# Latent attention: q up-projection in six full column tiles, rope on whole tiles, rope rows moved through memory

## Chip, cores, metric

The kernel runs on one core of a Trainium2 chip. The metric is the device time of one execution in microseconds (us). Three timed runs of the kernel before gave 1356.15, 1357.79 and 1358.18 us (median 1357.79). Engines: PE (TensorE) multiplies matrices into PSUM; DVE (VectorE), ACT (ScalarE) and POOL (GpSimd) work on elements; SP only issues DMAs here.

## The reference

One decoder block on x (1024 x 1024, float32): RMSNorm, one input projection, sliding-window attention A, latent attention B, gates and output projections, a residual, and a SwiGLU feed-forward. The change touches only B:

```python
cq = rmsnorm(q_lat, q_norm_g[l])                              # (S, 384)
qb = (cq @ w_uq[l]).reshape(B, S, MLA_HEADS, MLA_QK_DIM)      # 8 heads x 96
q_nope, q_rope = jnp.split(qb, [MLA_NOPE_DIM], axis=-1)       # 64 + 32
q_rope = apply_rope(q_rope, cos_b, sin_b)
ckv = rmsnorm(kv_lat, kv_norm_g[l])
kvb = (ckv @ w_ukv[l]).reshape(B, S, MLA_HEADS, MLA_NOPE_DIM + MLA_V_DIM)
k_nope, vb = jnp.split(kvb, [MLA_NOPE_DIM], axis=-1)
k_rope = apply_rope(k_r[:, :, None, :], cos_b, sin_b)[:, :, 0, :]   # one for all heads
o_b = mla_attention(q_nope, q_rope, k_nope, k_rope, vb)       # causal, scale 96 ** -0.5

def apply_rope(x, cos, sin):
    x1, x2 = jnp.split(x, 2, axis=-1)
    return jnp.concatenate([x1 * cos - x2 * sin, x2 * cos + x1 * sin], axis=-1)
```

## The kernel before, in words

**Arithmetic.** Every float32 operand of a matmul is kept as two parts, hi (rounded by ACT, L163) and lo = value - hi (DVE or POOL, L166), and a product is three matmuls (`mm3`, L172 to L174): hi by hi, hi by lo, lo by hi. One matmul has 128 x 128 weights and up to 512 moving columns.

**Stages.** Input projections; sixteen steps of sliding-window attention with the gate projection beside them; the latent attention; output projections with gates; `w_out`; the feed-forward. The change lies in the latent attention, from the last gate steps (L1049 on) to the last latent head.

**Latent attention before.** The normalised latents `lat` are transposed into `cq` (three tiles of 128 latent columns) and `ckv` (two). The rotated key part `krT` is copied into rows 64 to 127 of the three rotating key tiles `kT`; it stands there twice, in rows 64 to 95 and again in rows 96 to 127 (L692 to L695 write it twice). A head's 96 query columns are widened on the host to 128: 64 plain ones, the 32 rope ones, and the 32 rope ones with their halves swapped (`_layouts`, L1714). `prod_q(h, s)` (L1090) makes q of one head and one half s of the sequence: nine matmuls, one DVE multiplication by the table `rope_t` (1 in the plain rows, cos in rows 64 to 95, -sin and +sin in rows 96 to 127, all times the scale), then hi on ACT and lo on POOL. The score matmul over 128 rows adds the cos and the sin products, since the key stands twice. `prod_k(j, s)` (L1100) makes the plain key of two heads, `prod_v(b)` (L1111) v of all heads for one block.

**Order.** Before the loop: `prod_q(0, 0)`, `prod_q(0, 1)`, `prod_k(0, 0)`, `prod_k(0, 1)`, `scores(0)`, and eight `prod_v` with `scores(1)` after the fourth. The loop runs over 64 tiles t (8 heads x 8 query blocks, the blocks of a head in the order 2, 3, 6, 7, 0, 1, 4, 5; n = t mod 8 is the place in that order): `scores(t + 2)`, then `pv` of a pair that is due, then at n = 2 and 4 the two halves of `prod_q(h + 1)`, at n = 3 and 5 of odd heads the two halves of `prod_k((h + 1) // 2)`, then `transposes(t)`. `scores` (L1132) writes a PSUM tile of two banks (`scb`, two of them), DVE takes the row bound, ACT the exponential p, POOL the reciprocal and the scaling of p; `transposes` (L1159) turns p on PE into `pTb`, and ACT and DVE split it to `pth` and `ptl`; `pv` (L1174) multiplies with v. So q and k of later heads are PE work between the softmax steps of the current one. Late in the loop (t from 30 on) parts of the next stage are mixed in: `load_oa`, `split_oa`, `split_ob`, weights, and in the last head `mix_a`.

**Who decides the order.** Up to L1036 PE and SP follow the program as written. From there to the middle of the `w_out` stage a planner sets the order of each engine's instructions at compile time, by program order and by which operands and buffers it expects to be ready. At run time each engine and each DMA queue goes strictly in that order.

**Buffers.** `U` is a pool of 21 slots of 4 KB per partition (weights' raw and split tiles, p, pth, ptl, tables), `V` one of 17 slots of 8 KB (`cq`, `ckv`, `kT`, `vM`, `qT`, later `oaT`), `P1` four PSUM banks (q, k, v, pTb, ob, oA), `PX` the other four (gate sums, then the two score tiles). A new tile waits until the last reader of the slot's former tile is done. Weights come through a `Stream`: `load_to` issues the DMA, `conv_to` splits, `get` takes the tiles.

Of the kernel before, what the change touches and what calls it, by code (L numbers as in the profile page):

```python
# [8 lines left out]
F32 = mybir.dt.float32  # L9
# [8 lines left out]
P = 128  # L18
# [24 lines left out]
C_RT = QL  # L43
C_CKV = QL + 2 * ROPE_B
LAT = C_CKV + KVL
# [44 lines left out]
def hybrid_block_kernel(  # L90
# [94 lines left out]
    def half(s):  # L185
        return slice(512 * s, 512 * s + 512)
# [18 lines left out]
    h_d = dram.tile([NB, P, 2, 4, P], F32, name="h_d")  # L205
    q_d = dram.tile([2 * NB, P, 256], F32, name="q_d")
    lat_d = dram.tile([NB, P, LAT], F32, name="lat_d")
    gate_d = dram.tile([16, P, S], F32, name="gate_d")
# [47 lines left out]
    def uq_unit(j):  # L256
        def load():
            raw = U("wr", F32, (P, 2, 3, P))
            nc.sync.dma_start(raw, w_uq[j])
            return raw  # L260

        def conv(raw):
            ws = []
            for u in range(2):
                w = U("wuq", F32R, (P, 2, 3, P))
                split(w[:, 0], w[:, 1], raw[:, u])
                ws.append(w)
            return ws

        st.add(("uq", j), load, conv)  # L270

    uq_unit(0)
    wkv2 = []

# [16 lines left out]
    for k in range(2):  # L291
        ukv_unit(k)
    for j in range(1, 4):
        uq_unit(j)
    for nm, dp in (("oa", 0), ("oa", 1), ("oa", 2), ("ob", 0), ("ob", 1), ("oa", 3), ("ob", 2), ("ob", 3)):
# [97 lines left out]
    def halves(ap, hw):  # L393
        return ap.rearrange("p (h t d) -> p h t d", t=2, d=hw)
# [670 lines left out]
    gate_step()  # L1065
    rope_t = U("rope_t")
    nc.sync.dma_start(rope_t, c_rope_t)
    st.conv_to(st.index[("ukv", 1)])
    gate_step()
    kT = [hi_lo("kT") for _ in range(3)]  # L1070
    for s in range(2):
        pr = P1("krT", (HD, 4, P))
        for j in range(4):
            nc.tensor.transpose(pr[:, j], lat[4 * s + j][:, C_RT:C_CKV], ident)
        for hi, lo in kT:
            split(hi[64:128, half(s)], lo[64:128, half(s)], pr.rearrange("p b c -> p (b c)"))
    gate_step()
# [3 lines left out]
    wk, wv = wkv2  # L1081
    wuq = {0: st.get(("uq", 0))}

# [5 lines left out]

    def prod_q(h, s):  # L1090
        if s == 0:
            qT[h] = hi_lo("qT")
        w = wuq[h // 2][h % 2]
        ps = P1("q")
        mm3(ps, [((w[:, 0, k], w[:, 1, k]), (cq[k][0][:, half(s)], cq[k][1][:, half(s)])) for k in range(3)])
        qf = U("qf")
        nc.vector.tensor_tensor(qf[:, 0:512], ps, rope_t[:, half(s)], op=ALU.mult)
        split(qT[h][0][:, half(s)], qT[h][1][:, half(s)], qf[:, 0:512], nc.gpsimd)

    def prod_k(j, s):  # L1100
# [3 lines left out]
        for u in range(2):  # L1104
            hi, lo = kT[(2 * j + u) % 3]
            split(hi[0:64, half(s)], lo[0:64, half(s)], ps[64 * u:64 * u + 64])

    prod_q(0, 0)
    prod_q(0, 1)

    def prod_v(b):  # L1111
# [5 lines left out]
        split(vM[b][:, :, 0:HD], vM[b][:, :, HD:P], ps.rearrange("p (h d) -> p h d", d=HD))  # L1117

    prod_k(0, 0)
    prod_k(0, 1)  # L1120

# [149 lines left out]
    for t in range(NT):  # L1271
# [429 lines left out]
def _layouts(a):  # L1701
# [6 lines left out]
    def pairs(m):  # L1708
# [4 lines left out]
    uq = a["w_uq"].reshape(3, P, NH, QK)  # L1713
    uq = np.concatenate([uq, uq[..., 80:96], uq[..., 64:80]], axis=-1)  # L1714
    out = [("x", a["x"]), ("x_t", a["x"].reshape(NB, P, NK, P).transpose(0, 3, 2, 1)),
# [3 lines left out]
           ("w_kl", tiles(w[:, C_KVL:C_KR])), ("w_gt", pairs(w[:, C_GATE:])), ("sinks", a["swa_sinks"]),  # L1719
           ("q_g", a["q_norm_g"]), ("w_uq", uq.reshape(3, P, 4, 2, P).transpose(2, 1, 3, 0, 4)),  # L1720
           ("kv_g", a["kv_norm_g"]), ("w_ukv", a["w_ukv"])]
# [8 lines left out]
def _constants():  # L1730
# [13 lines left out]

    rt = np.concatenate([np.ones((64, S), np.float32), c.T, c.T, -s.T, s.T]).astype(np.float32) * np.float32(-SC_B)
    q = np.arange(P)[:, None]
# [35 lines left out]
```

## Time and profile before

| | before |
|---|---|
| median of three timed runs | 1357.79 us |
| profiled execution, first to last instruction | 1357.9 us |
| mean granted PE clock | 0.999 |
| instructions | 18990, of them 6600 matmuls |
| latent attention, first q matmul to last score matmul | 350.9 to 543.7 us |
| bytes moved by DMA | 202.25 MB |

In the lists of instructions each row has the start in us, the duration in us, engine, line, operation, output<-input, shapes, and in brackets the idle time of the engine just before it and what ended that. A matmul of 512 columns is listed with some 390 ns, but the next one starts about 226 ns later: it is the distance of starts that counts for PE. In the table by stretches, each engine's busy time is followed by the number of its instructions. Rows of a tile give minimum, median and maximum duration in ns.

### The profile page before, as it was taken

What the parts mean: (1) busy time and instruction counts of PE and PEld (TensorE: products, weight loads), DVE (VectorE), ACT (ScalarE), POOL (GpSimd) and SP (SyncE); (2) the same over time, 40 slices, a digit from 0 to 9 for tenths busy, and PEclk for the clock granted to TensorE, in tenths of its full rate; (3) what the DMA queues carried; (4) which work ended last, traced back from release to release, by engine and by line L of the source; (5) the groups of instructions that cost most, each with busy time, mean ns of one, the idle gap of its engine ahead of it and who ended that gap; (6) DMA issues with size and microseconds to landing.
All of it is one profiled execution on the core that took longest, in us unless ns stands there. A gap on an engine that the chain in (4) does not pass through costs nothing.

```text
span 1357.9 us, 18990 instructions
## 1 busy us (share of the span) xinstructions
PE 1338.8 (99%) x6600; PEld 1122.6 (83%) x6600; DVE 914.3 (67%) x1495; ACT 641.1 (47%) x1299; POOL 557.1 (41%) x610
## 2 busy tenths in 40 slices
PE   9999999999999999999999999999999999999997
PEld 6899878878888888888887888888888888888886
DVE  6868767776777787585448866666656654664862
ACT  7433767665567777651336232322332332644443
POOL 1115545553166554200031465766665551022521
PEclk9999999999999999999999999999999999999999
DMA  9454322335100110671243353644434425996504
GB/s 359 162 182 157 115 102 83 101 129 179 54 1 13 44 47 17 250 239 55 112 167 134 127 175 143 228 178 178 151 137 178 164 85 180 380 380 245 171 11 145
DMA packets 78239, 202.25 MB, mean 149 GB/s; under 512 B 8768, under 2 KB 15424, under 8 KB 78144
## 3 DMA queue, kind: packets, MB, share of 16 engines
q1 hardware_dynamic: 76704, 198.68, 41.2%
q10 hardware_dynamic: 1440, 2.36, 0.5%
q8 instruction: 52, 0.85, 0.2%
q14 instruction: 43, 0.35, 0.1%
HBM read 141.24 MB, written 59.77 MB: 148 GB/s over the span
## 4 chain that ended last, share of the span: by engine, by line
PE 79%; DVE 8%; ACT 4%; issue 3%; POOL 3%; DMA 2%; SPq 0%; POOLq 0%; ACTq 0%; DVEq 0%
PE fa L174 7%; PE fa L172 7%; PE fa L173 7%; PE fb L174 6%; PE fb L173 6%; PE fb L172 6%; PE fd L172 5%; PE fd L174 5%; PE fd L173 5%; PE xo L172 2%; PE xo L174 2%; PE xo L173 2%; PE pTb L1170 1%; PE oA L172 1%; PE oA L174 1%
## 5 line engine op out<-in xcount | busy, mean ns | idle before, releaser
L166 DVE TENSOR_TENSOR wl<-wr,wl 128x512 fp32r<-128x512 f32 x150 | 153.6, 1048 | 72.3 <-ACT wl L163 71.9
L166 DVE TENSOR_TENSOR lrv<-lr,lrv 128x1024 fp32r<-128x1024 f32 x77 | 104.9, 1396 | 48.6 <-ACT lrv L163 44.5
L163 ACT CAST lrv<-lr 128x1024 fp32r<-128x1024 f32 x77 | 80.1, 1052 | 94.1 <-PE fd L174 55.6
L172 PE MATMUL fd<-lrv 128*128 128x512 f32 x308 | 119.8, 389 | 0.0
L173 PE MATMUL fd<-lrv 128*128 128x512 f32 x308 | 119.8, 389 | 0.0
L174 PE MATMUL fd<-lrv 128*128 128x512 f32 x308 | 119.8, 389 | 0.0
L177 POOL TENSOR_TENSOR wr<-wr,sm 128x512 f32<-128x512 f32 (+1 forms) x38 | 46.4, 1229 | 150.8 <-DVE wl L166 117.2
L163 ACT CAST wl<-wr 128x512 fp32r<-128x512 f32 x150 | 86.9, 623 | 2.1 <-DVE wr L828 1.9
L304 POOL TENSOR_SCALAR ms<-ss 128x1 f32<-128x1 f32 x32 | 8.7, 271 | 189.8 <-ACT xn L1546 111.5
L166 DVE TENSOR_TENSOR wl<-sm,wl 128x512 fp32r<-128x512 f32 x60 | 47.2, 812 | 46.0 <-ACT wl L163 45.9
L174 PEld LDWEIGHTS fd<-lrv 128*128 128x128 f32 x308 | 57.8, 188 | 12.1
L173 PEld LDWEIGHTS fd<-lrv 128*128 128x128 f32 x308 | 57.8, 188 | 12.1
L172 PEld LDWEIGHTS fd<-lrv 128*128 128x128 f32 x308 | 57.8, 188 | 11.8
L1155 POOL TENSOR_TENSOR denb<-denb,neg_one 128x1 f32<-128x1 f32 x64 | 38.0, 594 | 69.2 <-ACT p L1154 56.8
L1154 ACT ACTIVATE p<-scb,nmb 128x384 f32<-128x384 f32 (+3 forms) x64 | 47.6, 744 | 38.4 <-DVE nmb L1153 36.5
L166 DVE TENSOR_TENSOR ptl<-pTb,pth 128x512 fp32r<-128x512 f32 (+2 forms) x96 | 50.5, 550 | 14.0 <-ACT pth L163 13.4
L1153 DVE CUSTOM_DVE_ANT_0 scb<-scb,mask 128x384 f32<-128x384 f32 (+3 forms) x64 | 48.5, 758 | 13.1 <-PE scb L1145 12.5
L1438 ACT ACTIVATE act<-sm 128x512 f32<-128x512 f32 x11 | 7.0, 633 | 104.9 <-DVE sm L180 104.9
L1156 POOL TENSOR_SCALAR p<-p,denb 128x384 f32<-128x384 f32 (+3 forms) x64 | 49.4, 773 | 6.3
L163 ACT CAST pth<-pTb 128x512 fp32r<-128x512 f32 (+2 forms) x96 | 43.3, 482 | 12.2 <-PE pTb L1170 11.6
L172 PE MATMUL fb<-t2h,wl 128*128 128x512 f32 x120 | 47.4, 395 | 0.0
L172 PE MATMUL fb<-t3h,wl 128*128 128x512 f32 x120 | 47.3, 394 | 0.0
(348 smaller groups left out, 4310.2 us busy)
## 6 DMA issues: line engine op xcount, KB each, us to landing
lr<-la_d SPq DMA_DIRECT2D x77, 256.0 KB, 5.4
wr<-in_w_gate_dram SPq DMA_DIRECT2D x22, 512.0 KB, 3.9
wr<-in_w_up_dram SPq DMA_DIRECT2D x22, 512.0 KB, 5.1
wd<-in_w_down_dram SPq DMA_DIRECT2D x22, 512.0 KB, 6.6
rb_d<-wd SPq DMA_DIRECT2D x22, 512.0 KB, 2.6
la_d<-sd SPq DMA_DIRECT2D x22, 512.0 KB, 5.3
lr<-rb_d SPq DMA_DIRECT2D x44, 256.0 KB, 5.4
lr<-in_w_down_dram SPq DMA_DIRECT2D x33, 256.0 KB, 5.8
```

Of the source, the lines that this page charges most:

```text
L163: i = nc.scalar.copy(hi, src)
L166: (eng or nc.vector).tensor_tensor(lo, src, hi.bitcast(F32), op=ALU.subtract)
L172: nc.tensor.matmul(ps, ah, bh, start=first and i == 0, stop=False, skip_group_check=go_on)
L173: nc.tensor.matmul(ps, ah, bl, start=False, stop=False, skip_group_check=go_on)
L174: nc.tensor.matmul(ps, al, bh, start=False, stop=last and i == n - 1, skip_group_check=go_on)
L177: eng.tensor_tensor(out, a, b, op=ALU.subtract)
L304: nc.gpsimd.tensor_scalar(ms, ss, 1.0 / width, EPS, op0=ALU.mult, op1=ALU.add)
L1153: nc.vector.tensor_tensor_reduce(s_, s_, m_, 1.0, -NEG, op0=ALU.add, op1=ALU.min, accum_out=nm)
L1154: nc.scalar.activation(p_, s_, AF.Exp, scale=-1.0, bias=nm, accum_out=den)
L1155: nc.gpsimd.tensor_tensor(den, den, neg_one[:, 0:1], op=ALU.pow)
L1156: nc.gpsimd.tensor_scalar(p[:, 0:w], p[:, 0:w], den, 0.0, op0=ALU.mult, op1=ALU.add)
L1170: nc.tensor.transpose(pp[:, i], p[:, blk(k0 + i)], ident)
```

## The change

The eight widened column tiles of the q up-projection become six full ones: two tiles (`w_rope`) hold the first and the second rope half of all eight heads (8 x 16 columns each), four hold the plain 64 columns of two heads each. Four `uq` units of weights become three; two of them are taken before the loop.

A new function `prod_rope(s)` computes the two rope tiles for a half of the sequence (two times nine matmuls), multiplies each on DVE by a cos and a sin table (two table tiles instead of one), subtracts and adds on POOL, splits into hi and lo (ACT, DVE), and stores them to a new buffer `qr_d` in device memory. `prod_q(j, s)` now makes the plain part of two heads: nine matmuls, hi with the scale on ACT, lo on DVE, 64 rows each. At s = 0 it also issues four DMAs, two for each head, that fetch the head's 2 x 16 rope rows from `qr_d` into rows 64 to 95 of its `qT`. Scores use 96 rows instead of 128; the key's rope part stands once.

The order before the loop becomes: `prod_rope(0)`, `prod_rope(1)`, `prod_k(0, 0)`, `prod_k(0, 1)`, `prod_q(0, 0)`, `prod_q(0, 1)`, five `prod_v`, `scores(0)`, three `prod_v`, `scores(1)`. In the loop `prod_q` runs at n = 2 and 4 of heads 0, 2 and 4 only.

```diff
-C_CKV = QL + 2 * ROPE_B
+C_CKV = QL + ROPE_B
...
+    qr_d = dram.tile([2, P, 2, S], F32, name="qr_d")
...
     uq_unit(0)
+    uq_unit(1)
...
     for k in range(2):
         ukv_unit(k)
-    for j in range(1, 4):
-        uq_unit(j)
+    uq_unit(2)
...
-        kr = t[:, C_RT:C_CKV].rearrange("p (u d) -> p u d", u=2)
-        rope_nat(halves(ps[:, QL:416], 16), 1, 16, rope_b[:, 0, b], rope_b[:, 1, b],
-                 [kr[:, 0:1].rearrange("p h (t d) -> p h t d", t=2)])
-        nc.vector.tensor_copy(kr[:, 1], kr[:, 0])
+        rope_nat(halves(ps[:, QL:416], 16), 1, 16, rope_b[:, 0, b], rope_b[:, 1, b], [halves(t[:, C_RT:C_CKV], 16)])
...
-    rope_t = U("rope_t")
-    nc.sync.dma_start(rope_t, c_rope_t)
+    rope_t = [U("rope_t") for _ in range(2)]
+    for i in range(2):
+        nc.sync.dma_start(rope_t[i], c_rope_t[i])
...
-    wuq = {0: st.get(("uq", 0))}
+    w_rope = st.get(("uq", 0))
+    wuq = [None] * 4
+    wuq[0:2] = st.get(("uq", 1))
...
-    def prod_q(h, s):
-        if s == 0:
-            qT[h] = hi_lo("qT")
-        w = wuq[h // 2][h % 2]
+    def prod_rope(s):
+        ps = [P1("q") for _ in range(2)]
+        for w, p in zip(w_rope, ps):
+            mm3(p, [((w[:, 0, k], w[:, 1, k]), (cq[k][0][:, half(s)], cq[k][1][:, half(s)])) for k in range(3)])
+        c, d = U("qr", F32, (P, 2, 512)), U("qr", F32, (P, 2, 512))
+        for i in range(2):
+            nc.vector.tensor_tensor(c[:, i], ps[i], cos_t[:, half(s)], op=ALU.mult)
+            nc.vector.tensor_tensor(d[:, 1 - i], ps[i], sin_t[:, half(s)], op=ALU.mult)
+        sub(c[:, 0], c[:, 0], d[:, 0], nc.gpsimd)
+        add(c[:, 1], c[:, 1], d[:, 1], nc.gpsimd)
+        t = V("qrs", F32R, (P, 2, 2, 512))
+        for i in range(2):
+            split(t[:, i, 0], t[:, i, 1], c[:, i])
+            nc.sync.dma_start(qr_d[i][:, :, half(s)], t[:, i].bitcast(F32))
+
+    def prod_q(j, s):
+        for u in range(2):
+            if s == 0:
+                t = V("qT", F32R, (P, 2, S))
+                qT[2 * j + u] = (t[:, 0], t[:, 1])
+                for i in range(2):
+                    nc.sync.dma_start(t[64 + 16 * i:80 + 16 * i].bitcast(F32), qr_d[i, 16 * (2 * j + u):16 * (2 * j + u + 1)])
+        w = wuq[j]
         ps = P1("q")
         mm3(ps, [((w[:, 0, k], w[:, 1, k]), (cq[k][0][:, half(s)], cq[k][1][:, half(s)])) for k in range(3)])
-        qf = U("qf")
-        nc.vector.tensor_tensor(qf[:, 0:512], ps, rope_t[:, half(s)], op=ALU.mult)
-        split(qT[h][0][:, half(s)], qT[h][1][:, half(s)], qf[:, 0:512], nc.gpsimd)
+        for u in range(2):
+            hi, lo = (v[0:64, half(s)] for v in qT[2 * j + u])
+            p = ps[64 * u:64 * u + 64]
+            nc.scalar.activation(hi, p, AF.Copy, scale=-SC_B)
+            nc.vector.scalar_tensor_tensor(lo, p, -SC_B, hi.bitcast(F32), op0=ALU.mult, op1=ALU.subtract)
...
+    prod_rope(0)
+    prod_rope(1)
+    prod_k(0, 0)
+    prod_k(0, 1)
     prod_q(0, 0)
     prod_q(0, 1)
+    del w_rope
...
-        qh, ql = qT[h]
-        kh, kl = kT[h % 3]
+        qh, ql = (v[0:QK] for v in qT[h])
+        kh, kl = (v[0:QK] for v in kT[h % 3])
...
-    psum_phase("psb", 2)
-    scores(0)
     for b in range(NB):
+        if b == 5:
+            psum_phase("psb", 2)
+            scores(0)
         prod_v(b)
-        if b == 3:
-            scores(1)
+    scores(1)
...
-        if n == 0 and h % 2 == 0 and h + 2 < NH:
-            st.load_to(st.index[("uq", h // 2 + 1)])
-        if n == 0 and h % 2 == 1 and h + 1 < NH:
-            wuq[(h + 1) // 2] = st.get(("uq", (h + 1) // 2))
+        if t == 0:
+            st.load_to(st.index[("uq", 2)])
+        if t == NB:
+            wuq[2:4] = st.get(("uq", 2))
         if h + 1 < NH:
-            if n in (2, 4):
-                prod_q(h + 1, n // 2 - 1)
+            if n in (2, 4) and h % 2 == 0 and h + 2 < NH:
+                prod_q(h // 2 + 1, n // 2 - 1)
...
-    uq = np.concatenate([uq, uq[..., 80:96], uq[..., 64:80]], axis=-1)
+    uq = np.concatenate([uq[..., 64:80], uq[..., 80:96], uq[..., 0:64]], axis=-1)
+    uq = [uq[..., 16 * i:16 * i + 16].reshape(3, P, 1, P) for i in range(2)] + [uq[..., 32:].reshape(3, P, 4, P)]
+    uq = np.concatenate(uq, axis=2).reshape(3, P, 3, 2, P)
```

More of the change, by code (lines that the diff above doesn't have):

```diff
@@ L1071, in hybrid_block_kernel @@
     for s in range(2):
-        pr = P1("krT", (HD, 4, P))
+        pr = P1("krT", (ROPE_B, 4, P))
         for j in range(4):
@@ L1075, in hybrid_block_kernel @@
         for hi, lo in kT:
-            split(hi[64:128, half(s)], lo[64:128, half(s)], pr.rearrange("p b c -> p (b c)"))
+            split(hi[64:QK, half(s)], lo[64:QK, half(s)], pr.rearrange("p b c -> p (b c)"))
     gate_step()
@@ L1117, in prod_v @@
         split(vM[b][:, :, 0:HD], vM[b][:, :, HD:P], ps.rearrange("p (h d) -> p h d", d=HD))
-    prod_k(0, 0)
-    prod_k(0, 1)
     ob = {}
@@ L1719, in _layouts @@
            ("w_kl", tiles(w[:, C_KVL:C_KR])), ("w_gt", pairs(w[:, C_GATE:])), ("sinks", a["swa_sinks"]),
-           ("q_g", a["q_norm_g"]), ("w_uq", uq.reshape(3, P, 4, 2, P).transpose(2, 1, 3, 0, 4)),
+           ("q_g", a["q_norm_g"]), ("w_uq", uq.transpose(2, 1, 3, 0, 4)),
            ("kv_g", a["kv_norm_g"]), ("w_ukv", a["w_ukv"])]
@@ L1743, in _constants @@
     c, s = tables(ROPE_B)
-    rt = np.concatenate([np.ones((64, S), np.float32), c.T, c.T, -s.T, s.T]).astype(np.float32) * np.float32(-SC_B)
+    rt = np.stack([np.tile(c.T, (NH, 1)), np.tile(s.T, (NH, 1))]) * np.float32(-SC_B)
     q = np.arange(P)[:, None]
```

1 line of the change is left out of this document (added).

## The prediction

> **What bounds the kernel now.** I read the page first (busy shares, chain of waits), then the busy time by stretches, then the engines' instructions in the latent attention one by one.
>
> ```profile
> span 1357.9 us, 18990 instructions
> ...
> PE 1338.8 (99%) x6600; PEld 1122.6 (83%) x6600; DVE 914.3 (67%) x1495; ACT 641.1 (47%) x1299; POOL 557.1 (41%) x610
> ...
> PE 79%; DVE 8%; ACT 4%; issue 3%; POOL 3%; DMA 2%; SPq 0%; POOLq 0%; ACTq 0%; DVEq 0%
> ```
>
> PE is the bound of the whole, but 99% busy doesn't say that each matmul removed is won: a fifth of the chain runs through other engines. The stretches of the latent attention follow, the seven long ones cut where each head's block 4 starts its scores (the pairs of 320-column matmuls, one in each head).
>
> ```profile
> 340.00:350.00 10.00, 10.00 (x54) 8.41 (x53) 9.96 (x17) 6.63 (x14) 0.00 (x0) 1.00 0.28 101
> 350.00:360.00 10.00, 9.95 (x44) 7.84 (x43) 7.35 (x13) 5.14 (x10) 2.54 (x2) 1.00 0.22 74
> 360.00:370.00 10.00, 10.00 (x45) 8.27 (x45) 6.60 (x12) 5.62 (x12) 2.41 (x4) 1.00 0.00 0
> ...
> 378.69:400.76 22.07, 21.32 (x139) 18.70 (x138) 16.30 (x35) 15.16 (x36) 14.29 (x20) 1.00 0.01 2
> 400.76:422.18 21.42, 21.41 (x140) 18.61 (x138) 16.52 (x34) 14.97 (x35) 11.89 (x19) 1.00 0.06 19
> 422.18:444.21 22.03, 21.25 (x139) 18.65 (x138) 16.62 (x38) 15.42 (x37) 14.20 (x19) 1.00 0.00 1
> 444.21:465.64 21.43, 21.40 (x139) 18.64 (x138) 16.42 (x33) 14.98 (x35) 11.90 (x19) 1.00 0.22 68
> 465.64:488.10 22.46, 21.48 (x139) 18.65 (x138) 19.38 (x42) 17.15 (x41) 15.29 (x19) 1.00 0.08 24
> 488.10:510.18 22.08, 21.65 (x140) 18.68 (x138) 17.85 (x37) 15.89 (x36) 11.68 (x18) 1.00 0.16 49
> 510.18:537.66 27.48, 25.79 (x161) 22.52 (x159) 21.87 (x44) 19.51 (x44) 15.19 (x18) 1.00 0.07 21
> ```
>
> Columns: stretch, us, then PE, weight load, DVE, ACT, POOL, granted clock, DMA share, GB/s. PE is full up to 370; in the heads it idles 0.0 to 1.0 us of 22, most where DVE is busiest (19.38 of 22.46). DVE is also full from 340 to 350.
>
> **PE work: removed and added.** The starts of matmuls give a matmul's real price.
>
> ```profile
> 350.88 0.39 PE L172 MATMUL q<-cq,wuq 128*128 128x512 f32 x1
> ...
> 352.69 0.39 PE L174 MATMUL q<-cq,wuq 128*128 128x512 f32 x1
> 353.13 0.50 PE L172 MATMUL q<-cq,wuq 128*128 128x512 f32 x1
> ...
> 370.05 0.39 PE L174 MATMUL v<-wv,ckv 128*128 128x512 f32 x1
> 370.27 0.39 PE L1143 MATMUL scb<-kT,qT 128*128 128x512 f32 x1
> ```
>
> Eight steps take 352.69 - 350.88 = 1.81 us: 0.226 us each in a run of equal ones. In the heads nine q matmuls last from 394.32 to the next operation at 396.45 (rows below): 2.13 us, 0.237 each. Before, q costs 8 x 18 = 144 matmuls, 18 of them ahead of the loop and 18 in each of heads 0 to 6. After, it is 36 + 72 = 108: 54 ahead of the loop, 18 in heads 0, 2 and 4, none in heads 1, 3, 5, 6. So the loop loses 72 (4 x 2 x 2.13 = 17.0 us) and the front gains 36 (36 x 0.226 = 8.1 us). Net PE work: -8.9 us. Score matmuls keep their number and their columns, but use 96 rows instead of 128:
>
> ```profile
> 340.90 1.03 PE L1046 MATMUL lT<-ident,lat 128*128 128x128 f32 x8
> ...
> 347.24 1.03 PE L1074 MATMUL krT<-ident,lat 128*64 128x128 f32 x8
> ```
>
> No row varies the rows; the nearest varies the array's other side, and 128*64 takes the same 1.03 as 128*128. I price the rows at nothing. (Were they paid in proportion, 288 matmuls of about 0.2 us would lose a quarter, 14 us; the two equal rows exclude that for me.)
>
> **What of the 17.0 us is won.** Fewer matmuls only help while PE is what ends last. Element work of the heads hardly changes:
>
> ```profile
> L1097 DVE TENSOR_TENSOR qf<-q,rope_t x16: 672/691/693, 354.6 to 515.3; 128x512 f32<-128x512 f32 x16
> L163 ACT CAST qT<-qf 128x512 fp32r<-128x512 f32 x16 | 10.0, 622 | 5.2 <-DVE qf L1097 5.2
> L166 POOL TENSOR_TENSOR qT<-qf,qT x16: 1273/1290/1307, 356.0 to 517.9; 128x512 fp32r<-128x512 f32 x16
> L163 ACT CAST kT<-k 64x512 fp32r<-64x512 f32 x16 | 9.3, 580 | 2.4 <-PE k L174 1.3 <-DVE kT L166 0.7
> L166 DVE TENSOR_TENSOR kT<-k,kT 64x512 fp32r<-64x512 f32 x16 | 11.0, 686 | 3.7 <-ACT kT L163 3.5
> ```
>
> One half s of q of two heads cost DVE 2 x 0.69, ACT 2 x 0.62, POOL 2 x 1.29 before; after, two 64-row hi's and two 64-row lo's, priced by the k rows: DVE 2 x 0.69, ACT 2 x 0.58, POOL nothing. So DVE keeps its 16.4 us a stretch while PE falls to 21.4 - 2.13 = 19.3. What waits then shows in head 1:
>
> ```profile
> 389.24 0.33 PE L1143 MATMUL scb<-kT,qT 128*128 128x384 f32 x1
> ...
> 390.36 1.08 DVE L1153 CUSTOM_DVE_ANT_0 scb<-scb,mask 128x896 f32<-128x896 f32 x1
> ...
> 391.60 1.01 ACT L1154 ACTIVATE p<-scb,nmb 128x896 f32<-128x896 f32 x1 [1.16 <-DVE nmb L1153]
> ...
> 393.43 1.39 POOL L1156 TENSOR_SCALAR p<-p,denb 128x896 f32<-128x896 f32 x1
> ...
> 394.32 0.45 PE L172 MATMUL q<-cq,wuq 128*128 128x512 f32 x1
> ...
> 396.45 0.92 PE L1170 MATMUL pTb<-ident,p 128*128 128x128 f32 x7
> ...
> 396.21 1.12 POOL L1156 TENSOR_SCALAR p<-p,denb 128x1024 f32<-128x1024 f32 x1
> ```
>
> p of the 896-column block is scaled at 393.43 + 1.39 = 394.82, and PE, once the q matmuls in front are gone, wants to transpose it at 394.32: 0.5 us and a handover that I set at 0.2, so 0.7 us of the 4.26 come back as a wait in heads 1, 3 and 5. The next block's p comes 2.5 us later (396.21 + 1.12 = 397.33); in odd heads k covers that. Head 6 has neither q nor k after the change: of the 2.5 PE fills 1.2 (the seven transposes, a small score), so 0.7 + 1.3 = 2.0 us wait there. The stretch from 465.64 holds 1.1 us of splits that move away (two of 0.57, row below) and goes to PE 19.3 beside DVE 18.2; at the 86 to 88% that DVE reaches there now it ends after 20.9, a gain of 1.5 less the 0.7 of head 5's wait in the same stretch. The last (27.48, DVE 21.87) I lower by 1.4 of 2.13. By stretch: 1.4, 2.1, 1.4, 2.1, 0.8, 2.3, 1.4: 11.5 us won. Bounds: 17.0 (no waits), and 6 (if DVE's 16.4 can't pass 81% of a stretch, as in the one from 488.10, the first four stretches last 20.2 each, 81 instead of 87, and the last three win nothing).
>
> **The front, from 350.88.** It grows by 8.1 us of PE. Besides:
>
> ```profile
> 352.39 0.69 DVE L180 TENSOR_TENSOR go<-fa,pu 128x512 f32<-128x512 f32 x1
> ...
> L166 DVE TENSOR_TENSOR wuq<-wr,wuq x8: 553/568/1281, 341.0 to 481.9; 128x384 fp32r<-128x384 f32 x8
> L166 DVE TENSOR_TENSOR wl<-wr,wl 128x512 fp32r<-128x512 f32 x150 | 153.6, 1048 | 72.3 <-ACT wl L163 71.9
> ...
> oa_d<-oa SPq DMA_DIRECT2D x4, 512.0 KB, 2.9
> ...
> qn<-q_d SPq DMA_DIRECT2D x16, 128.0 KB, 2.9
> ```
>
> (a) A second unit of q weights is split before ukv: two DVE operations of 0.57 while DVE is full, so `go`, whose PSUM bank the second q tile waited for (352.69 to 353.13 instead of 0.23), comes 1.1 us later; 0.7 of it shows. (b) From there DVE has 8 rope products of 0.69, 4 lo's from SBUF of 1.05, 8 lo's of k and q of 0.69, 8 of v of 0.69, two bounds of some 0.7: 22.2 us, in a PE stretch of 19.4 + 8.1 = 27.5 that begins with 4 us of older DVE work. That is 95%, with four PSUM banks between PE and DVE: 1.2 us, bounds 0 and 4. For the lo's the skill has a rule against the change: a DVE operation with two SBUF inputs and a GpSimd operation that reads SBUF block each other entirely (Trainium skill, "SBUF — State Buffer", section "Who interferes with whom"). The p row above, 1.39 us beside two DVE splits, agrees with it; by the rule in full the four lo's would be 4 x (0.69 + 1.29), 3.7 us more than by the 1.05 row, and (b) would near its upper bound. (c) The rope rows: the last rope matmul ends near 360.0; products 2 x 0.69, POOL 2 x 1.29, hi 0.62, lo 1.05 and 0.7 of queueing give 366.3; store 0.3 + 2.9, 369.5; load 0.7 + 2.9, 373.1. PE reaches `scores(0)` after 36 + 12 + 18 + 30 matmuls, 350.88 + 21.7 + 0.2 + 0.7 + 1.2 = 374.7. Covered by 1.6 us; price 0, and if the 16-partition loads took 4 us more, 2.4. Front: 8.1 + 0.7 + 1.2 = 10.0 us.
>
> **The rest.** `V` has 17 slots. At t = 34 `prod_q(3, 0)` asks for two `qT` beside cq 3, ckv 2, kT 3, wk 1, vM 4, two live `qT`, one `oaT`: 18. The second waits until head 4's last scores, three tiles on, and a PSUM bank may wait with it: 0.4 us, bounds 0 and 3. The 16 loads and 4 stores pass SP's queue: the later loads are issued 12 tiles (some 30 us) before their scores, which hides a 3 us transfer even behind several others. Removed besides: eight key copies at 95 to 127 us under PE's work, one 384 KB weight load: nothing.
>
> Sum: -11.5 + 10.0 + 0.4 = -1.1, on the execution's 1357.9 (0.1 above the median): **1356.8 us**. Own range 1353.5 to 1360.
>
> **Rivals.** *PE stays the bound* (the planner pulls `pv`, k or scores into the holes): 17.0 won less 1.5 in head 6, front 9.5: -6.0, 1351.9. For it: stretches of 21.4 us without any idle PE. Against: the 0.5 us hole computed above. *The front's round trip decides*: the rope rows land after PE has run out of v (all 114 matmuls issued by about 379). Then the first softmax, whose steps (0.6, 0.8, 1.2 us and their delays, about 3.3 us together) v covers now, stands bare as well: 2.4 + 3.3 on top of the forecast, +4.6, 1362.5. It decides once the rows land later than 378.8, 5.7 us after my estimate. For it: in-order queues on DVE, POOL and SP, each with one more hop. Against: 1.6 us of slack and 18 more v matmuls behind that. If PE idled for over 3 us there, the skill's rule ("TensorE: Matmul & The Clock Gate", "Why this matters for your kernels") says that the clock falls back; here the granted clock is 1.00 in every stretch, and no row shows such a gap. *The heads are DVE-bound at once*: only 6 us won, the V slots cost 2: +6, 1363.9. That the change doesn't do what it says (PE work not falling by 36 matmuls) I exclude: the count is in the code.
>
> **Chances.** A measurement tells 0.2%, 2.7 us, from no change. Forecast 0.40 (of it 0.13 faster, 0.24 within, 0.03 slower), PE-bound 0.27 (faster), round trip 0.22 and DVE-bound 0.11 (slower): faster 0.40, same 0.24, slower 0.36. Range 1350.5 to 1363.5.
>
> **What would show it.** 6564 matmuls instead of 6600. Right: `scores(2)` starts 10 us later than 370.27 with PE full before it; odd heads last some 3.5 us less; new short waits of the transposes for POOL's p in heads 1, 3, 5, 6. Wrong: PE idle before `scores(0)` with the `qT` DMA as its releaser (round trip); heads 1, 3, 5 shorter by all of 4.26 (PE-bound); waits of v for PSUM banks above 1.2 us; PE waits near t = 34 to 37.

## The result

The kernel after takes 1359.80 us (median of 20 runs, 1357.40 to 1364.05), the kernel before, run beside it, 1357.61 us (20 runs, 1356.15 to 1360.17). The ratio is 1.0016, 95% interval 1.001 to 1.0023: **2.2 us slower**, where the prediction had 1.1 us faster.

The page of the kernel after, its first lines and the shares of the chain of waits:

```profile
span 1356.5 us, 18954 instructions
...
PE 1332.3 (98%) x6564; PEld 1115.4 (82%) x6564; DVE 913.7 (67%) x1497; ACT 643.1 (47%) x1301; POOL 540.2 (40%) x598
...
PE 84%; DVE 5%; POOL 4%; issue 4%; ACT 2%; DMA 0%; POOLq 0%; ACTq 0%; DVEq 0%
```

PE executes the 36 matmuls fewer, and yet the time grew. The span, 1356.5, is shorter than the 1357.9 of before, which seems to contradict the medians. The stages ahead of the latent attention decide that: the first q matmul starts at 350.88 in the profiled execution of before, at 347.81 in that of after, and a second execution of each (e1, e2 below) has 347.71 and 350.23. So the start moves by 3 us from one execution to the next of the same kernel. Behind that start the executions repeat within 0.1 us, and there the kernels differ:

| us | before | before, again | after | after, again |
|---|---|---|---|---|
| span | 1357.9 | 1354.6 | 1356.5 | 1359.0 |
| first q matmul | 350.88 | 347.71 | 347.81 | 350.23 |
| from there to the first `oA` (output projection) | 172.69 | 172.60 | 174.64 | 174.63 |
| from there to the first `xo` (`w_out`) | 274.51 | 274.43 | 276.47 | 276.46 |

The change costs 2.0 us between its first q matmul and the first `oA`, and nothing behind that. "By the trace" below means the distance from the first q matmul to the first `xo` in the profiled execution; it repeats within 0.1 us in the two kernels that were profiled twice, where the interval of a ratio is about 1 us to either side. The front, up to the start of `scores(2)`, grew from 19.39 us (350.88 to 370.27) to 29.17 (347.81 to 376.98), by **9.8**; the loop from there to `oA` fell from 153.30 to 145.47, by **7.8** instead of 11.5. The stretches of the loop after the change (columns as before), cut at the same scores, with a first row from `scores(2)` to the first cut, and the whole loop in each kernel:

```profile
376.98:385.98 9.00, 7.76 (x47) 6.32 (x45) 6.23 (x14) 6.29 (x15) 4.96 (x7) 1.00 0.13 30
385.98:406.62 20.64, 19.38 (x126) 16.67 (x124) 16.15 (x37) 14.29 (x34) 10.69 (x18) 1.00 0.06 14
406.62:426.91 20.29, 20.22 (x133) 17.33 (x131) 16.39 (x35) 15.58 (x37) 10.38 (x17) 1.00 0.05 14
426.91:447.86 20.95, 20.05 (x135) 17.23 (x133) 16.37 (x37) 15.47 (x36) 10.30 (x16) 1.00 0.06 14
447.86:467.11 19.25, 19.11 (x127) 16.55 (x125) 15.35 (x34) 14.15 (x34) 10.26 (x16) 1.00 0.26 69
467.11:487.80 20.69, 18.23 (x120) 15.41 (x118) 17.00 (x36) 14.97 (x36) 8.87 (x14) 1.00 0.08 26
487.80:508.19 20.39, 19.40 (x125) 16.49 (x125) 17.84 (x37) 15.81 (x37) 10.24 (x17) 1.00 0.16 53
508.19:536.56 28.37, 25.56 (x157) 21.78 (x157) 21.64 (x45) 20.13 (x44) 14.55 (x19) 1.00 0.06 20
376.98:522.45 145.47, 135.61 (x870) 115.57 (x868) 117.51 (x247) 107.79 (x247) 74.19 (x112) 1.00 0.10 28
```

```profile
370.27:378.69 8.42, 8.17 (x50) 6.78 (x49) 6.27 (x15) 5.74 (x13) 4.04 (x6) 1.00 0.01 2
...
370.27:523.57 153.30, 148.38 (x941) 129.03 (x940) 121.80 (x252) 109.95 (x251) 92.40 (x124) 1.00 0.08 24
```

PE's idle time in the loop doubled, from 153.30 - 148.38 = 4.92 to 145.47 - 135.61 = 9.86 us. DVE keeps nearly all its load (121.80 to 117.51).

These stretches show where PE idles, but their lengths can't be compared one by one, because the planner moved work across their ends. For example, six matmuls of the last k stand ahead of the cut at 488.10 before the change and behind the one at 487.80 after it; eight transposes stand ahead of 510.18 before, and behind 508.19 after. So the last stretch is 0.9 us longer than before partly because it holds these transposes. Cut instead at the first `ob` matmul (L1192 before, L1218 after) behind the block-4 scores, each stretch holds the same matmuls in both kernels, but for q and for one score matmul that stands on the other side of 409.10. The last one ends at the first `oA`:

| from, before | from, after | us before | us after | q matmuls | won |
|---|---|---|---|---|---|
| 370.27 | 376.98 | 9.38 | 10.41 | 9 and 9 | -1.0 |
| 379.65 | 387.39 | 22.07 | 21.71 | 18 to 9 | 0.4 |
| 401.72 | 409.10 | 21.42 | 19.42 | 18 to 9 | 2.0 |
| 423.14 | 428.52 | 22.03 | 20.30 | 18 to 9 | 1.7 |
| 445.17 | 448.82 | 21.44 | 19.90 | 18 to 9 | 1.5 |
| 466.61 | 468.72 | 22.46 | 22.65 | 18 to 9 | -0.2 |
| 489.07 | 491.37 | 22.07 | 19.02 | 18 to 0 | 3.1 |
| 511.14 | 510.39 | 12.43 | 12.06 | 9 to 0 | 0.4 |

Nine q matmuls hold 2.1 us. "By `ob` cuts" below means these stretches; the second profiles of both kernels repeat them within 0.05 us.

In the last of them the instructions show how so little was won. First after the change, then before, with PE's start of the scores of the 640-column block, DVE's work and bound for it, and what PE did meanwhile:

```profile
509.50 0.40 PE L1169 MATMUL scb<-kT,qT 96*128 96x320 f32 x1
...
510.85 0.56 DVE L166 TENSOR_TENSOR ptl<-pTb,pth 128x384 fp32r<-128x384 f32 x1 [0.63 <-ACT pth L163]
511.32 0.68 DVE L166 TENSOR_TENSOR wv<-oar,wv 128x512 fp32r<-128x512 f32 x1
511.92 1.28 DVE L166 TENSOR_TENSOR ptl<-pTb,pth 128x512 fp32r<-128x512 f32 x2
...
513.12 1.22 DVE L166 TENSOR_TENSOR wl<-wr,wh 128x1024 fp32r<-128x1024 f32 x1
...
514.25 0.82 DVE L1179 CUSTOM_DVE_ANT_0 scb<-scb,mask 128x640 f32<-128x640 f32 x1
...
517.72 0.77 PE L1196 MATMUL pTb<-ident,p 128*128 128x128 f32 x5 [0.74 <-POOL p L1182]
...
520.11 0.66 PE L1196 MATMUL pTb<-ident,p 128*128 128x128 f32 x4 [0.94 <-POOL p L1182]
```

```profile
510.70 0.31 PE L1143 MATMUL scb<-kT,qT 128*128 128x320 f32 x1
...
512.04 0.45 PE L172 MATMUL q<-cq,wuq 128*128 128x512 f32 x1
...
513.93 0.39 PE L174 MATMUL q<-cq,wuq 128*128 128x512 f32 x1
...
514.55 0.82 DVE L1153 CUSTOM_DVE_ANT_0 scb<-scb,mask 128x640 f32<-128x640 f32 x1
...
521.22 0.66 PE L1170 MATMUL pTb<-ident,p 128*128 128x128 f32 x4 [1.69 <-POOL p L1156]
```

The scores are there at about 510.2, but in DVE's queue the bound stands behind splits of the next stage (`wv`, `wl`) and of `pTb`, and starts at 514.25, 4.75 us after the start of the last three score matmuls. Before, it was late too (514.55 - 510.70 = 3.85), but nine q matmuls (512.04 to 514.16) lay under it. Without them PE comes to the transposes early and waits for POOL's p, which follows the bound. From the first `ob` on to `oA` PE idles 1.69 us in one wait before the change, 2.58 in four after it (two of them are the last rows of the first list).

### The profile page after: what moved, and what is told of

Same layout as the page of the kernel before. It is cut to its first block, busy times and chain, and to the rows that moved or that the text cites. A ratio compares the mean times of both kernels' runs of the same rounds, so it can differ in the third digit from the quotient of the medians.

```text
span 1356.5 us, 18954 instructions
## 1 busy us (share of the span) xinstructions
PE 1332.3 (98%) x6564; PEld 1115.4 (82%) x6564; DVE 913.7 (67%) x1497; ACT 643.1 (47%) x1301; POOL 540.2 (40%) x598
## 4 chain that ended last, share of the span: by engine, by line
PE 84%; DVE 5%; POOL 4%; issue 4%; ACT 2%; DMA 0%; POOLq 0%; ACTq 0%; DVEq 0%
PE fa L174 7%; PE fa L172 7%; PE fa L173 7%; PE fb L174 6%; PE fb L172 6%; PE fb L173 6%; PE fd L173 5%; PE fd L172 5%; PE fd L174 5%; PE xo L172 2%; PE xo L174 2%; PE xo L173 2%; POOL p L1182 2%; POOL denb L1181 1%; PE pTb L1196 1%
## 5 line engine op out<-in xcount | busy, mean ns | idle before, releaser
L166 DVE TENSOR_TENSOR wl<-wr,wl 128x512 fp32r<-128x512 f32 x150 | 148.5, 1014 | 72.3 <-ACT wl L163 72.0
L1196 PE MATMUL pTb<-ident,p 128*128 128x128 f32 x288 | 45.9, 278 | 5.9 <-POOL p L1182 4.9
L1464 ACT ACTIVATE act<-pu 128x512 f32<-128x512 f32 x22 | 13.9, 633 | 70.5 <-DVE pu L180 70.5
```

Of the source, the lines that this page charges most:

```text
L166: (eng or nc.vector).tensor_tensor(lo, src, hi.bitcast(F32), op=ALU.subtract)
L1196: nc.tensor.transpose(pp[:, i], p[:, blk(k0 + i)], ident)
L1464: nc.scalar.activation(dst, src, AF.Silu)
```

## The experiments

Three theories. **A**: the front costs what was forecast, and the loop wins less, because q had filled waits of PE that stay. **B**: the round trip of the rope rows through memory decides. **C**: something ahead of the latent attention changed. All timed runs beside the kernel before on the same chip:

| run | median, us | ratio to before | by the trace, us |
|---|---|---|---|
| e1 before again | 1357.77 | 0.9999 [0.999, 1.0007] | 274.43 |
| e2 after again | 1359.58 | 1.0011 [1.0002, 1.002] | 276.46 |
| e3 rope rows from an early copy | 1358.95 | 1.0011 [1.0002, 1.002] | 277.31 |
| e4 the same without rope work | 1352.17 | 0.9951 [0.9938, 0.9963] | (see there) |
| e5 before, head 6's q left out | 1355.35 | 0.9983 [0.9974, 0.9991] | 272.68 |
| e6 before, head 1's q left out | 1355.70 | 0.9982 [0.9973, 0.9991] | 270.97 |
| e7 after, output products in head 6 | 1357.67 | 1.0001 [0.9992, 1.001] | 275.26 |
| e8 after, low halves on POOL | 1356.02 | 0.9988 [0.9979, 0.9997] | 274.14 |
| e9 after, q spread | 1361.21 | 1.0026 [1.0015, 1.0038] | 280.04 |
| e10 after, e7 + e8 + e9 | 1356.81 | 0.9998 [0.9989, 1.0007] | 274.93 |
| e11 before, low halves on POOL | 1359.05 | 1.0012 [1.0003, 1.0021] | 275.90 |
| e12 after, q matmuls twice in head 6 | 1357.81 | 1.0005 [0.9996, 1.0014] | 275.54 |
| e13 after, e7 + e8 | 1355.55 | 0.998 [0.9972, 0.9989] | 272.22 |
| e14 before, output products in head 6 | 1357.67 | 0.9993 [0.9984, 1.0002] | 274.54 |

**e1 and e2: both kernels again.**

> The kernel before, once more, for a second profile of it. The profiled execution after began its first q matmul at 347.8 us, the one before at 350.9, although the code ahead differs only by eight small copies. Theory A (the loss lies in the latent attention: the front costs about 9.8 us more, the heads win only about 7.8): the start of the first q matmul varies from execution to execution by some 3 us, and the stretch from first q matmul to the first oA matmul repeats at 172.7 us within 0.5. Theory C (the change moves something ahead of the latent attention): this profile starts its first q matmul at 350.9 within 0.5 again. Ratio to before 1.000 within 0.001.

> The changed kernel once more. Theory A: first q matmul to first oA matmul 174.6 us within 0.7, that is 1.9 more than before; ratio to before 1.0016 within 0.001. Theory B (the rope rows' way through memory decides, and varies with the DMAs): the stretch from the first q matmul to the first score matmul differs by over 1 us from the 23.85 us of the first profile, and PE idles ahead of the first score matmul.

The table above holds them: the difference in the latent attention is there each time, the difference ahead of it comes and goes with the execution, for both kernels. C falls.

**e3 and e4: the round trip, and the rope work.** e3 loads a head's rope rows from a buffer that is filled from `cq[0]` before `prod_rope`; the rope products and their stores stay, so only the scores' dependence on them is gone. e4 also leaves out both calls of `prod_rope`.

```diff
+    early_d = dram.tile([P, 2, S], F32, name="early_d")
...
-                    nc.sync.dma_start(t[64 + 16 * i:80 + 16 * i].bitcast(F32), qr_d[i, 16 * (2 * j + u):16 * (2 * j + u + 1)])
+                    nc.sync.dma_start(t[64 + 16 * i:80 + 16 * i].bitcast(F32), early_d[16 * (2 * j + u):16 * (2 * j + u + 1)])
...
+    for i in range(2):
+        nc.sync.dma_start(early_d[:, i], cq[0][i].bitcast(F32))
-    prod_rope(0)
-    prod_rope(1)
```

(The last two lines are e4's alone.)

> The changed kernel, with the rope rows of every head fetched from a buffer that holds the first latent tile, stored before prod_rope starts; the rope work and its stores stay. The rope values that the scores use are therefore others. Nothing then waits for products, POOL, splits and store. Theory A: same time as the changed kernel within 1 us (the round trip is covered by k, q and v work). Theory B: 2 to 5 us faster than the changed kernel.

> As the run with rows fetched early, but the two prod_rope calls are left out altogether: 36 matmuls, 8 products, 4 POOL operations, 4 hi's, 4 lo's and 4 stores fewer. Theory A: 9 to 10 us faster than the changed kernel (8.1 us of PE and 1 to 2 us of waits for PSUM banks), near 1350. If PE's work in the front were hidden: less than 5 us faster. Theory B: over 11 us faster.

e3 is not faster than after; by the trace it is 0.8 us slower, 0.6 of that in its front (24.48 us from the first q matmul to the first score against 23.85). B falls. The kernel after says the same: the two loads for which the first scores wait landed at 369.01 and 370.65, and the first score matmul starts at 371.66. Its DMA issues (size and us to landing) and PE's waits:

```profile
qr_d<-qrs SPq DMA_DIRECT2D x4, 512.0 KB, 3.4
qT<-qr_d SPq DMA_DIRECT2D x16, 128.0 KB, 3.3
```

```profile
359.38 0.47 PE L172 MATMUL q<-cq,wuq 128*128 128x512 f32 x1 [0.18 <-DVE qr L1100]
364.70 0.47 PE L172 MATMUL v<-wv,ckv 128*128 128x512 f32 x1 [0.96 <-DVE kT L166]
...
371.66 0.34 PE L1169 MATMUL scb<-kT,qT 96*128 96x384 f32 x1
```

The first score matmul has no idle time in front of it; what PE waits for in the front are PSUM banks that DVE frees. e4 has its k products ahead of q, so its trace is taken from the start of the last gate matmul to the first `oA`: 166.4 us, against 174.9 in after and 172.9 in before. The rope work costs 8.5 us by this (7.4 between the medians of e2 and e4), less than the 9 to 10 expected: e4's own front has a wait that after's doesn't have, 1.51 us of its first q matmul for a bank that DVE's split of k frees. The loop behind is the same without rope work, to 0.1 us a stretch by `ob` cuts: the two parts of the loss are separate.

**e5 and e6: what q is worth where it stood.** In the kernel before, one head's q is left out.

```diff
-            if n in (2, 4):
+            if n in (2, 4) and h == 6:
+                qT[7] = qT[6]
+            elif n in (2, 4):
                 prod_q(h + 1, n // 2 - 1)
```

(e6: `h == 1` and `qT[2] = qT[1]`.)

> The kernel before, without the 18 q matmuls of head 6 (qT[7] is qT[6]: head 7 computes head 6's attention again). It asks what PE work is worth in the last stretch, alone, without the change. Theory A (head 6 is set by the chain of scores, bound, exp, scaling and transposes, and by DVE, which has the next stage's weight splits in front of the bounds; the q matmuls only filled its waits): at most 1 us faster than before, and the waits of pTb for POOL's p and of scores for the score tile grow there by what the q matmuls filled. Rival (PE is the bound there, and my 1.4 us failed through something that the change adds): 18 x 0.237 = 4.3 us, less at most 0.7.

> The kernel before, without the 18 q matmuls of head 1 (qT[2] is qT[1]). The same question for an odd head, where the prediction takes 4.26 - 0.7 = 3.5 us won, and the kernel after showed 1.1 + 1.1 in the two halves of it that lie in different stretches. Theory A (a hole of the softmax chain behind each half of q that is taken out): 2.2 us faster than before. Rival, the prediction's own price: 3.5 us.

e5 wins 1.8 us by the trace of the 4.3 that its 18 matmuls hold, between the two forecasts. By `ob` cuts the stretch with the first nine takes 20.94 us instead of 22.07, the one with the second nine 11.73 instead of 12.43: 1.1 and 0.7 won of 2.1 each. More than half of these 18 matmuls was filler: PE work that lies under a wait for something else. e6 wins 3.5 us by the trace, the prediction's own price, so theory A's 2.2 was wrong for an odd head taken by itself. By `ob` cuts the two halves are 1.5 and 1.8, against 0.4 and 2.0 in the kernel after (not 1.1 + 1.1). Both runs also take q's work away from DVE, ACT and POOL, which the change only moves to the even heads; whether that makes e6's difference from after, no run shows.

**e7, e8, e13: give head 6 something to do, or take DVE's work away.** e7 puts two products of the next stage between head 6's blocks; e8 makes the low halves of `oar` (`wv` above) on POOL; e13 has both.

```diff
-    early = {0: (0, 0), 1: (1, 0), 3: (0, 1), 4: (1, 1), 5: (2, 0), 6: (2, 1), 7: (3, 0)}
+    early = {-5: (0, 0), -3: (1, 0), 3: (0, 1), 4: (1, 1), 5: (2, 0), 6: (2, 1), 7: (3, 0)}
...
-        if e == -6:
+        if e == -8:
             st.conv_to(st.index[("oa", 0)])
```

```diff
-        split(hi[:, c], lo[:, c], raw[:, c])
+        split(hi[:, c], lo[:, c], raw[:, c], nc.gpsimd)
```

> The kernel after, with two of the next stage's first output products (mix_a of tiles 0 and 1, and the conversion that feeds them) put between head 6's blocks, ahead of where they stood. If PE idles in head 6 only because nothing ready stands in its queue (theory A): 1 to 3 us faster than after, and the waits of pTb and scores shrink by as much. If DVE sets the pace of head 6 itself: 0 to 0.5 us, the work only changes place.

> The kernel after, with the low halves of the converted attention output made on POOL instead of DVE: DVE loses some 1.05 us for each chunk in and behind the heads, POOL (at 40%) takes 1.3 for each. If DVE's place ahead of the bounds is what holds head 6 (theory A): 0.5 to 2 us faster than after. If the chain's own length sets it: 0, or up to 1 us slower, since POOL also scales p.

> The kernel after with two of the edits, without the spread of q that made it slower: two output products between head 6's blocks, and the low halves of the converted attention output on POOL. By the traces the kernel with all three edits took 154.7 us from head 5's block-4 scores to the first xo, and the one with the low halves alone 154.9: both edits are for the same hole. So 0 to 1 us faster than the low halves alone, 2.3 to 3.3 us faster than after by the trace, and 0.4 to 1.4 us faster than before by it. If the gains of the two add where q isn't spread: 3.5 us faster than after.

e7 wins 1.2 us by the trace, e8 2.3 us (0.3 above its forecast), e13 4.25, more than the sum: my expectation of one hole for both was wrong. In e8 the bound of the 640-column block comes 3.41 us behind the start of its last three score matmuls (4.75 in after), for `wv` is gone from DVE's queue ahead of it, and the last stretch by `ob` cuts is 0.6 us shorter (11.47 against 12.06). Rows of e8:

```profile
507.78 0.31 PE L1169 MATMUL scb<-kT,qT 96*128 96x320 f32 x1
...
508.66 1.30 POOL L166 TENSOR_TENSOR wv<-oar,wv 128x512 fp32r<-128x512 f32 x1 [1.32 <-ACT wv L163]
...
511.19 0.82 DVE L1179 CUSTOM_DVE_ANT_0 scb<-scb,mask 128x640 f32<-128x640 f32 x1
```

The larger part of e8's gain lies in head 5, in the stretch that takes 22.65 us in after and 20.43 in e8 (the next one is 0.5 longer). There e8's planner also set six k matmuls ahead of the block-4 scores, where after has them behind. e12 below has that order without e8's edit, and takes 21.21. So up to 1.4 us of e8's gain may come from the order; the runs don't separate it from the relief of DVE.

e13 is faster than both kernels, 2.1 us by the medians and 2.3 by the trace against before.

**e11 and e14: the same two edits in the kernel before.**

> The kernel before, with the low halves of the converted attention output on POOL: what the relief of DVE is worth without the change. Theory A (in the kernel before, q matmuls fill the time in which DVE is late, so its relief brings less there than the 2.3 us of the trace that it brought in the kernel after): 0 to 1.2 us faster than before. Rival (DVE's lateness costs the same with and without the q matmuls): 2.3 us.

> The kernel before, with the same two output products put between head 6's blocks: the counterpart of the run that gave 1.2 us by the trace in the kernel after. Theory A (in the kernel before q already fills those waits): 0 to 0.4 us faster than before, or slower by up to 0.5. Rival (the output products find waits there in any case): 1.2 us faster.

e14 changes nothing by the trace (274.54 against 274.51), as theory A has it: with q in head 6, other products there win nothing. e11 is 1.4 us **slower** by the trace (0.8 by the medians); both expectations missed that. Its POOL queue in head 6 shows how it begins:

```profile
514.70 0.90 ACT L1154 ACTIVATE p<-scb,nmb 128x768 f32<-128x768 f32 x1 [0.30 <-DVE nmb L1153]
514.71 1.28 POOL L166 TENSOR_TENSOR qT<-qf,qT 128x512 fp32r<-128x512 f32 x1
...
515.95 1.29 POOL L166 TENSOR_TENSOR wv<-oar,wv 128x512 fp32r<-128x512 f32 x1
...
517.84 0.97 POOL L1156 TENSOR_SCALAR p<-p,denb 128x768 f32<-128x768 f32 x1
...
518.87 0.66 PE L1170 MATMUL pTb<-ident,p 128*128 128x128 f32 x4 [2.17 <-POOL p L1156]
```

p is there at 515.6, but POOL has q's low half and then the new one ahead of it, scales it at 517.84, and PE waits 2.17 us, 0.5 more than at the same place before (1.69). Most of the loss comes behind that wait: the granted PE clock (third number from the end) falls to 0.50 for 3.4 us while PE is busy.

```profile
516.71:518.87 2.16, 0.00 (x0) 0.00 (x0) 2.13 (x5) 1.50 (x4) 2.06 (x4) 1.00 0.00 0
519.69:523.10 3.41, 3.41 (x14) 3.03 (x13) 2.10 (x5) 2.72 (x7) 1.68 (x3) 0.50 0.00 0
```

From the score matmul at 519.29 to the first `oA` at 522.49 it takes 3.20 us, against 1.94 for the same matmuls before (521.63 to 523.57): 1.3 us. Without the fall of the clock e11 would be about as fast as before, by this estimate. The two edits are worth 0.0 and -1.4 us by the trace before the change, 1.2 and 2.3 after it; but as most of the -1.4 is the clock, it isn't shown that POOL became a place for others only because the change took q's low halves off it.

**e9 and e10: q spread over even and odd heads.**

```diff
-            if n in (2, 4) and h % 2 == 0 and h + 2 < NH:
-                prod_q(h // 2 + 1, n // 2 - 1)
+            if n == (4, 2)[h % 2] and h + 2 - h % 2 < NH:
+                prod_q(h // 2 + 1, h % 2)
```

> The kernel after, with q's second half of a pair moved from block 4 (in order of work) of the even head to block 2 of the odd head, and its first half from block 2 to block 4 of the even head: each of heads 0 to 5 then issues nine q matmuls instead of 18 and none. Nothing else changes, the PE work is the same. Theory A (in the odd heads PE idles behind the softmax chain where q no longer fills it, and the even heads are bound by PE): 1 to 2.5 us faster than after. Rival (the loss is only in head 6 and ahead of oA): 0 to 0.3 us.

> The kernel after with three edits together: q spread over even and odd heads, two output products between head 6's blocks, the low halves of the converted attention output on POOL. If the holes are separate, the gains add: by the trace from the first q matmul to the first xo 1.2 and 2.3 us for the last two, and 1 to 2.5 for the first, 4.5 to 6 us faster than after, 2 to 4 us faster than before. If head 6's two edits fill the same hole: 3.3 to 4.8 us faster than after.

A miss for both theories: e9 is 3.6 us slower than after by the trace. The odd heads' waits didn't close, a new one opened, of k for a PSUM bank that DVE's `ob` frees:

```profile
406.34 0.50 PE L172 MATMUL k<-ckv,wv 128*128 128x512 f32 x1 [1.20 <-DVE ob L1230]
```

The new half of q stands 4.6 us ahead of it, at 401.73, and takes one of the four `P1` banks, as k does. This row explains 1.2 us. Of the rest, most of which lies in heads 4 and 5, a part may again be the clock: e9's profiled execution has it at 0.50 from 479.57 to 482.99, in head 5, behind waits of 1.00 and 0.45 us, which can cost up to 1.7 us. By the ratios to before (1.0026, against 1.0016 and 1.0011 of the kernel after) e9 is 1.4 to 2.0 us slower than after. What causes the rest stays open. e10, with this edit among its three, wins 1.5 us against after by the trace, below both of its forecasts, and is 2.7 us slower than e13.

**e12: PE work alone.**

```diff
+        if h == 6 and n in (2, 4):
+            mm3(P1("q"), [((wuq[3][:, 0, k], wuq[3][:, 1, k]), (cq[k][0][:, half(n // 2 - 1)], cq[k][1][:, half(n // 2 - 1)])) for k in range(3)])
```

> The kernel after, with the 18 q matmuls of pair 3 issued a second time in head 6, at the blocks where the kernel before had its q, into a PSUM bank that nothing reads: PE work alone, no work on DVE, ACT or POOL. Theory A (PE idles there for want of ready work): of their 18 x 0.237 = 4.3 us less than half shows, 0 to 2 us slower than after by the trace from the first q matmul to the first xo, and the waits of pTb for POOL's p shrink. Rival (PE is the bound there and the waits seen are of no account): 3.5 to 4.3 us slower.

18 matmuls more, 4.3 us of PE work, and by the trace 0.9 us **less**, outside both forecasts. PE's waits from head 5's last blocks to the end of the heads (line, releaser, us in total, times, longest), first in after, then in e12:

```profile
PE pTb L1196 <- POOL p L1182: 3.2, 5, 0.9
PE ob L1219 <- DVE ptl L166: 0.9, 2, 0.7
PE scb L1169 <- ACT p L1180: 0.2, 1, 0.2
PE k L172 <- DVE ptl L166: 0.2, 1, 0.2
```

```profile
PE pTb L1196 <- POOL p L1182: 0.9, 2, 0.6
PE ob L1218 <- DVE ptl L166: 0.4, 2, 0.2
```

They fall from 4.5 to 1.3 us. That covers 3.2 of the 4.3, and not the gain. The planner orders the queues for the program as it finds it: in e12 PE's order differs from after's already in head 5 (there k stands ahead of the scores of block 4), so the run is not the bare addition that I meant. The `ob` cuts part the two. Head 5's stretch, the same matmuls in the other order, takes 21.21 us instead of 22.65: 1.4 won. What follows up to `oA`, with the 18 matmuls more, takes 19.95 + 11.69 = 31.64 instead of 19.02 + 12.06 = 31.08: 0.6 lost, of 4.3 us of added PE work, and nothing in the last stretch. So the gain is the other order's, and head 6 isn't bound by PE.

## Why the prediction was wrong

- **The front, +10.0: right in the sum.** It measured +9.8, 8.1 of it by 36 matmuls and 1.7 by waits for banks (1.9 forecast). Their places differ. The 0.7 for a later `go` doesn't show: the first matmul that had to wait stands 0.47 us behind the one ahead of it (351.66 to 352.13), against 0.44 before. The four banks, forecast 1.2, cost 1.5: 358.81 to 359.38 and 363.36 to 364.70 instead of 0.23 each, at the two waits in the rows above.
- **The rope lo's:** they took 3.6 us together, less than the 4 x 1.05 taken for them:

```profile
L166 DVE TENSOR_TENSOR qrs<-qr,qrs x4: 691/904/1118, 356.7 to 363.1; 128x512 fp32r<-128x512 f32 x4
```

  The row reads minimum, median, maximum in ns over four. Two of them, at 357.94 and 363.14, ran while POOL did nothing, and took 0.69 us. The two others, at 356.69 and 361.88, began 0.57 us before a POOL operation on `qr` ended, and took 1.12, that is 0.43 more. The rule of the Trainium skill ("SBUF — State Buffer", section "Who interferes with whom") that such DVE operations and GpSimd's exclude each other would make it 0.57 more, which is near. The full sum of 0.69 + 1.29 asks for two operations that begin together, and none did.
- **The round trip, 0: right**, by e3. The rows landed 22.8 us after the first q matmul (22.2 forecast), 1.0 us ahead of the first score matmul (1.6 forecast).
- **The `V` slots, +0.4: not seen.** The stretch that holds t = 34, 447.86 to 467.11, has 0.14 us of PE idle time, and the waits that follow it, from 477.36 on, are for p.
- **The score rows, 0: right.** Score matmuls of 320 columns start 0.15 apart with 96 rows (507.78 to 507.93 in e8) as with 128 (510.70 to 510.85 in before).
- **The loop, -11.5: the step that failed.** It measured -7.8: 3.7 us less was won, which is more than the whole distance of 3.3 between the forecast (-1.1) and the result (+2.2). By stretches, the sum's own terms beside the `ob` cuts:

| stretch, from | forecast won | won |
|---|---|---|
| 370.27 | 0 | -1.0 |
| 379.65 | 1.4 | 0.4 |
| 401.72 | 2.1 | 2.0 |
| 423.14 | 1.4 | 1.7 |
| 445.17 | 2.1 | 1.5 |
| 466.61 | 0.8 | -0.2 |
| 489.07 | 2.3 | 3.1 |
| 511.14 | 1.4 | 0.4 |

Four terms are 1.0 us too high each and one is 0.6 too high; the one from 489.07 is 0.8 too low, which was luck and hides a part of that.

The last term is "The last (27.48, DVE 21.87) I lower by 1.4 of 2.13". That took a part of the removed work as won because DVE was busy for only 80% of the stretch. What counts is DVE's order: the bound stands behind the splits, and the nine matmuls lay under that (taken away alone in e5 they win 0.7; put back in e12 they cost nothing). The profile of before showed it, q from 512.04 to 514.16 and the bound at 514.55.

The term from 466.61 (head 5) priced DVE's load and one wait. In the kernel after the planner set k behind the block-4 scores, and PE waits ahead of it:

```profile
477.36 0.50 PE L1169 MATMUL scb<-kT,qT 96*128 96x512 f32 x1 [1.12 <-ACT p L1180]
...
479.00 0.66 PE L1196 MATMUL pTb<-ident,p 128*128 128x128 f32 x4 [0.45 <-POOL p L1182]
...
486.45 0.98 PE L1196 MATMUL pTb<-ident,p 128*128 128x128 f32 x7 [0.80 <-POOL p L1182]
```

e12, with the same matmuls in the other order, is 1.4 us faster there, more than the 1.0 that the term missed.

The first two terms lie ahead of head 1's block 4. The sum has nothing for the loop's start. There `scores(0)` now comes after five `prod_v` and `scores(1)` after all eight, so that less PE work stands beside the first softmax steps; that this order is the cause, no run shows. In heads 1, 3 and 5 I counted one wait of 0.7 for POOL's p. PE's waits at the start and in head 1 of the kernel after are of three kinds, for a score tile that ACT still reads, for p, and for a split on DVE:

```profile
379.32 0.50 PE L1169 MATMUL scb<-kT,qT 96*128 96x512 f32 x1 [0.64 <-ACT p L1180]
385.56 0.66 PE L1196 MATMUL pTb<-ident,p 128*128 128x128 f32 x4 [0.60 <-POOL p L1182]
...
395.81 0.65 PE L1196 MATMUL pTb<-ident,p 128*128 128x128 f32 x4 [0.21 <-POOL p L1182]
399.05 0.50 PE L1169 MATMUL scb<-kT,qT 96*128 96x512 f32 x1 [0.27 <-ACT p L1180]
404.26 0.52 PE L1196 MATMUL pTb<-ident,p 128*128 128x128 f32 x3 [0.77 <-DVE ptl L166]
```

So the mechanism named, waits for POOL's p where q had covered them, came, but it was one of several: waits for score tiles and for DVE's splits came with it, and the planner's order of the rest, which the sum took as unchanged. In heads 5 and 6 the runs show the cause; ahead of head 1's block 4 it stays open. The rival by which the heads are DVE-bound at once was nearer on the loop (6 us won, 7.8 measured), but its sign, nothing won from 465.64 on, didn't come (2.6 by the scores' cuts, 3.2 by the `ob` cuts up to `oA`). The sum also has no term for a fall of the clock behind such waits, which some executions of the kernel after probably had (last section).

## What to carry to other kernels

Before PE work is counted as won, look at what stands behind it in time: if the next step that PE needs is late whether or not the work is there, the work is a filler and its removal wins little or nothing. That is read instruction by instruction in the stretch, not from an engine's share: DVE at 80% of a stretch held PE up because its queue had other work ahead of the one bound that mattered. When filler is taken away, look for what may take its place, and for an engine that the change relieved (here POOL): with two edits that try this, the loss of 2.2 us became a gain of 2.1 against before, though part of that may be the planner's order. And compare stretches of two kernels only between instructions that enclose the same work.

## What the runs showed besides

The first q matmul starts at 347.2 to 351.4 us in the profiled executions, without any order by kernel, and the same kernel takes the same time from there on, within 0.1 us as far as `xo`. A difference of 2 us between two kernels can't be read from two spans, but it can from the distance between two instructions inside a stage.

The granted clock fell to 0.50 for 3.4 us in the loop of four profiled executions, each time behind waits of PE: in e11 after one wait of 2.17 us, in e3, e7 and e9 in head 5 after waits of 1.12 (e9: 1.00) and 0.45 us that lie 1.2 us apart. So a gap of over 3 us, the condition in the prediction, wasn't needed. Nor do such waits always do it: the two profiles of the kernel after have the same 1.12 and 0.45 us without a fall. The fall cost 1.3 us in e11, but 0.1 in e7 (22.77 against 22.65 us in head 5's stretch by `ob` cuts), where PE was not what the stretch waited for. In the timed runs it can be seen only in the mean granted clock, where one such fall is 0.5 x 3.4 / 1357 = 0.0013: the mean is 0.9976 over the 20 runs of the kernel after and 0.9979 in e2, against 0.9988 in the runs of before beside e2. So the waits that the change opened probably cost some of its executions clock as well; how much of the 2.2 us that is, no run shows.
